# Merged heads stored as one word, and the last recurrent block's scans placed behind attention's first maxima

## The chip, the cores and the metric

The kernel runs on one core of a Trainium2 chip. The metric is device time in microseconds (us) of one execution; lower is better. A core has five engines, each with its own instruction queue that it works through in order: TensorE (PE in the profile, with its weight loads as PEld), VectorE (DVE), ScalarE (ACT), GpSimd (POOL) and SyncE (SP), which here only issues transfers. All transfers run on the core's 16 DMA engines.

## The reference, cut to what matters

One layer of a hybrid encoder over 16 + 1024 tokens of 1024 features. An attention branch (8 query heads of 128, 2 key/value heads) and a recurrent branch (8 blocks of 128 channels, scanned forward and backward) are gated, added, projected and added to the residual; a feed-forward follows.

```python
rnn = (rg_lru(xc, ..., reverse=False) + rg_lru(xc, ..., reverse=True))
rnn = rnn.astype(x.dtype) * jax.nn.gelu(gr)
attn = bidirectional_gqa(q, k, v)        # softmax(q k^T) v, 1024 queries over 1040 keys
g_attn, g_rnn = sigmoid(g_merge) halves
mix = g_attn * attn + g_rnn * rnn
h = h + mix @ w_out[l]
hn = rmsnorm(h, norm2_g[l])
h = h + (silu(g) * u) @ w_ffn_out[l]     # g, u = halves of hn @ w_ffn_in[l]
```

## The kernel before, in words

Fp32 products are made on TensorE from two words per number: `split` writes a rounded high word on ACT (a copy into fp32r, L96) and the low word, the difference, on DVE or POOL (L97). A product is then three matmuls (`mm3`, L102 to L104).

**Recurrent part.** A loop over 8 channel blocks makes projections, gates and decays, and calls `scans(b, ri, aa, tg)`: square roots on ACT (L501), then on DVE for each direction a product (L506) and a scan (L509), then the sum of both directions (L511) and the product with `tg` (L512), and a store to `rm_d[b]` in DRAM (L513). For the last block, b = 7, this is the last work on DVE ahead of attention, and `load_head(0)` has brought in the first query head (`qh`).

**Attention.** For head h and query tile i of 128 queries (64 tiles), `emit_scores` makes scores on PE in one of two PSUM buffers `S0`, `S1` (nine matmuls), their negated maximum `nm` on DVE (L585), the exponential `p` with its sum on ACT (L588), the reciprocal on DVE, and `PP`, the normalised tile as high and low fp16 words (ACT L594, L595; DVE L597). `PP` has a ring of 3 buffers. A DMA transpose, issued by SP (L600), brings `PP` into `PT`. Two tiles make a pair u; `emit_pv`, called up to two pairs later, runs 25 matmuls (`pv`, L611), multiplies by the attention gate on DVE (L613) and adds the recurrent part on POOL (L614), both in a page `gar` that `load_gar` filled from `rm_d`. The gate projections of the coming head (`gap`, L636 to L638) fill PE between score tiles.

**Merged heads.** `emit_pv` splits each 128x256 result into `mst` (ACT, POOL) and stores the two words to `mix_d` (256 KB, L618). `load_mix(kh, c)` later brings the two words of up to 4 heads and half of the tokens into pages `M`, two transfers issued by POOL (L650): four calls, two of them inside the last heads by the table `ahead`, two behind them. The first half of the output projection (`oph`, L677 to L679, with `load_wout` L656 and `load_h` L668 ahead of it) begins beside head 7, then the second half and the norm follow.

**What sets the order.** The code is recorded in this order and a scheduler places instructions on each engine; pools with rings (`pages`, a shared ring of page tiles; `rawp`, three staging tiles `raw`) give a buffer back when its last reader is done. SP issues transposes, loads and stores in one queue, in order: an instruction of SP that waits holds back all behind it.

Of the kernel before, what the change touches and what calls it, by code (L numbers as in the profile page):

```python
# [19 lines left out]
T = 1024  # L20
# [3 lines left out]
NH = 8  # L24
# [18 lines left out]
def tile_hybrid_encoder_block(  # L43
# [73 lines left out]
    rm_d = [dram.tile([128, T], F32, name=f"rm_d{b}") for b in range(NB)]  # L117
    mix_d = [dram.tile([2, 4, 128, T], F32, name=f"mix_d{kh}") for kh in range(2)]

# [377 lines left out]

    def scans(b, ri, aa, tg):
        for r in range(2):
            rr = ri[r][:, 0, (0 if r == 0 else NM):NK]  # L500
            S.activation(out=rr, in_=rr, func=AF.Sqrt)  # L501
        for r in range(2):
            p = ri[r]
            lo = 0 if r == 0 else NM
            rr, ii, a1 = p[:, 0, lo:NK], p[:, 1, lo:NK], aa[:, r, lo:NK]
            V.tensor_tensor(out=ii, in0=ii, in1=rr, op=ALU.mult)  # L506
            if r:
                rr, ii, a1 = rr[:, ::-1], ii[:, ::-1], a1[:, ::-1]
            V.tensor_tensor_scan(out=rr, data0=a1, data1=ii, initial=0.0, op0=ALU.mult, op1=ALU.add)  # L509
        hf, hb = ri[0][:, 0, NM:NK], ri[1][:, 0, NM:NK]  # L510
        V.tensor_tensor(out=hf, in0=hf, in1=hb, op=ALU.add)  # L511
        V.tensor_tensor(out=hf, in0=hf, in1=tg, op=ALU.mult)  # L512
        SP.dma_start(out=rm_d[b], in_=hf)  # L513
# [10 lines left out]
    for b in range(NB):  # L524
        sg = gm_project(b, next_block())
        tg = pb.tile([128, T], F32, name="tg")
        gr = gr_project(b, next_block(), sg, tg)
# [9 lines left out]
        else:  # L537
            q = load_head(0)
        scans(b, ri, aa, tg)

# [23 lines left out]
    SB = [ps2.tile([128, 3, 512], F32, name=f"S{i}") for i in range(2)]  # L564
    PP = [p2.tile([128, KPAIR], F16, bufs=1, name=f"PP{i}") for i in range(3)]
    for p in PP:
# [5 lines left out]
    def emit_scores(h, i, q):  # L572
# [3 lines left out]
        s = SB[n % 2]  # L576
        pair = PP[n % 3]
        if n < 2:
# [5 lines left out]
        nm = small.tile([128, 1], F32, name="nm")  # L584
        V.tensor_reduce(out=nm, in_=s[:, :, 0:KC], axis=AX.XY, op=ALU.max, negate=True)  # L585
        p = p2.tile([128, 3, KC], F32, name="p")
# [11 lines left out]
        if i % 2 == 0:  # L598
            PT[h, i // 2] = p2.tile([128, 17, 256], F16, name="PT")
        SP.dma_start_transpose(  # L600
            out=PT[h, i // 2][:, :, 128 * (i % 2):128 * (i % 2) + 128], in_=pair,
        )

    def emit_pv(h, u, gar):
# [9 lines left out]
        G.tensor_tensor(out=gar[:, 1, c], in0=gar[:, 0, c], in1=gar[:, 1, c], op=ALU.add)  # L614
        if h < NH - 1 or u >= 2:
            st = p2.tile([128, 2, 256], F32R, name="mst")
            split(gar[:, 1, c], st[:, 0], st[:, 1], G)
            SP.dma_start(out=mix_d[h // 4][:, h % 4, :, c].rearrange("l d t -> d l t"), in_=f32(st))  # L618
        elif u % 2 == 1:
            cs = slice(256 * u - 256, 256 * u + 256)  # L620
            split(gar[:, 1, cs], M[0][1][0][:, 3], M[1][1][0][:, 3])
# [22 lines left out]

    def load_mix(kh, c):

        k = 3 if kh and not c else 4
        for hl in range(2):
            M[hl][kh][c] = page([128, 4, 512], F32R, f"M{hl}{kh}{c}")
            G.dma_start(out=M[hl][kh][c][:, 0:k], in_=mix_d[kh][hl, 0:k, :, 512 * c:512 * c + 512].rearrange("h d t -> d h t"))  # L650

# [33 lines left out]
    def out_steps():  # L685
# [8 lines left out]
    ahead = {  # L694
        (6, 4): [(load_mix, 0, 0)],
        (6, 6): [(load_wout, 0, 0), (load_wout, 1, 0)],
        (6, 7): [(load_h, 0, page, [0])],
        (7, 2): [(load_h, 0, page, [1])],
        (7, 3): [(load_wout, 0, 1)],
        (7, 4): [(load_mix, 1, 0)],  # L700
        (7, 5): [(load_wout, 1, 1)],
# [3 lines left out]
    for h in range(NH):  # L705
        for i in range(8):
            emit_scores(h, i, q)
            if i == 1 and h + 1 < NH:
# [463 lines left out]
```

## Time and profile before

| | |
|---|---|
| time, median of 3 runs | 1540.17 us (1540.11 to 1542.09) |
| profiled run: its own time | 1543.0 us |
| its span, first to last instruction | 1541.2 us |
| mean granted TensorE clock | 0.988 |
| PE busy | 1484.2 us, 96% of the span |
| DVE, ACT, POOL busy | 71%, 48%, 21% |
| DMA, mean of the span | 150 GB/s |

PE is nearly always busy, so a microsecond is won only where PE stands idle or runs at its lower clock. In the page's 40 slices PE is full (9 tenths) in most; lower digits stand at the very start, around 500 us, between 690 and 810 us and around 900 us. The DMA row of the same slices reads 9 from about 540 to 810 us, which is attention, and 4 or less in most slices before.

### The profile page before, as it was taken

How to read it: one execution, taken by the hardware profiler on the slowest of the kernel's cores; microseconds unless marked ns; L12 is line 12 of the kernel's file. 1: busy time of each engine (PE TensorE's matmuls, PEld its weight loads, DVE VectorE, ACT ScalarE, POOL GpSimd, SP SyncE). 2: the span in 40 equal slices, each digit the busy share in tenths (PEclk: the TensorE clock that was granted, in tenths of full speed). 3: DMA queues.
4: the chain of work that ended last, by engine and by line, in shares of the span. 5: the costliest groups of instructions: out<-in, count | busy, mean ns of one | idle time of the engine just before them, and what ended most of it. 6: DMA issues, size and time to landing. Idle time of an engine off the chain costs nothing. (4 is left out here: it accounts for less than half of the span.)

```text
span 1541.2 us, 20211 instructions
## 1 busy us (share of the span) xinstructions
PE 1484.2 (96%) x7323; PEld 1241.6 (81%) x7323; DVE 1101.1 (71%) x1712; ACT 743.1 (48%) x1264; POOL 325.3 (21%) x243
## 2 busy tenths in 40 slices
PE   6999999999999899997889979999999999999999
PEld 4888888888888788886778857888888888788887
DVE  6888677777776777786764697777777777667562
ACT  5544476677667666666651352322222222364330
POOL 0000000000000544444341253333333333300000
PEclk9999999999999999999999989999999999999999
DMA  6123311122212799999997215444444444699641
GB/s 240 41 77 101 88 33 60 60 62 62 63 55 78 167 201 201 202 199 228 234 228 246 69 40 165 164 157 158 157 157 158 157 158 157 230 378 330 205 149 66
DMA packets 310196, 230.49 MB, mean 150 GB/s; under 512 B 151016, under 2 KB 252352, under 8 KB 310096
## 3 DMA queue, kind: packets, MB, share of 16 engines
q1 hardware_dynamic: 306128, 221.34, 50.9%
q0 software_dynamic: 3968, 7.86, 1.9%
q8 instruction: 57, 0.93, 0.2%
q14 instruction: 43, 0.35, 0.1%
HBM read 137.15 MB, written 56.36 MB: 126 GB/s over the span
## 5 line engine op out<-in xcount | busy, mean ns | idle before, releaser
L96 ACT ACTIVATE wS<-s 128x512 fp32r<-128x512 f32 x88 | 53.2, 628 | 169.2 <-DVE s L880 51.6
L597 DVE SCALAR_TENSOR_TENSOR PP<-p,pr,PP 128x1024 f16<-128x1024 f32 (+1 forms) x128 | 119.4, 986 | 20.2 <-ACT PP L594 20.0
L96 ACT ACTIVATE pw<-pr 128x1024 fp32r<-128x1024 f32 x77 | 81.0, 1061 | 104.8 <-PE po L1088 63.4
L1086 PE MATMUL po<-pw 128*128 128x512 f32 x308 | 120.4, 391 | 1.5 <-ACT pw L96 1.5
L1087 PE MATMUL po<-pw 128*128 128x512 f32 x308 | 120.6, 391 | 0.8 <-DVE pw L97 0.8
L1088 PE MATMUL po<-pw 128*128 128x512 f32 x308 | 120.3, 391 | 0.0
L97 DVE TENSOR_TENSOR pw<-pr,pw 128x1024 fp32r<-128x1024 f32 x77 | 94.0, 1251 | 36.1 <-ACT pw L96 29.7
L611 PE MATMUL pv<-PT,vt 128*128 128x256 f16 x800 | 97.7, 281 | 17.6 <-DMA PT<-PP 16.9
L588 ACT ACTIVATE p<-S,nm 128x1044 f32<-128x1044 f32 x64 | 72.2, 1129 | 68.2 <-DVE nm L585 65.7
L611 PEld LDWEIGHTS <-vt 128*128 128x128 f16 x800 | 78.0, 101 | 33.5 <-issue 18.3
L97 DVE TENSOR_TENSOR wS<-s,wS 128x512 fp32r<-128x512 f32 x88 | 70.5, 818 | 16.9 <-ACT wS L96 16.0
L594 ACT ACTIVATE PP<-p,pr 128x1040 f16<-128x1040 f32 x64 | 73.9, 1155 | 15.2 <-DMA PT<-PP 10.3
L585 DVE TENSOR_REDUCE nm<-S 128x1 f32<-128x1044 f32 x64 | 76.8, 1231 | 2.1 <-PE S L104 2.1
L433 POOL MEMSET xrp<- 128x2 f32 x8 | 0.9, 108 | 349.8 <-DVE xc L440 349.8
L102 PE MATMUL S<-kT,qh 128*128 128x348 f32 (+1 forms) x192 | 63.6, 331 | 6.7 <-ACT p L588 6.4
L1086 PEld LDWEIGHTS po<-pw 128*128 128x128 f32 x308 | 58.1, 189 | 14.1 <-ACT pw L96 1.9
L1087 PEld LDWEIGHTS po<-pw 128*128 128x128 f32 x308 | 58.2, 189 | 13.0 <-DVE pw L97 1.1
L1088 PEld LDWEIGHTS po<-pw 128*128 128x128 f32 x308 | 58.2, 189 | 12.2
L103 PE MATMUL S<-kT,qh 128*128 128x348 f32 (+1 forms) x192 | 62.1, 323 | 0.0
L104 PE MATMUL S<-kT,qh 128*128 128x348 f32 (+1 forms) x192 | 62.0, 323 | 0.0
L97 DVE TENSOR_TENSOR wA<-raw,wA 128x512 fp32r<-128x512 f32 x60 | 50.3, 842 | 15.9 <-ACT wA L96 15.9
L103 PE MATMUL xr<-xn,wblk 128*128 128x264 f32 (+1 forms) x192 | 61.4, 320 | 0.0
(308 smaller groups left out, 4467.0 us busy)
## 6 DMA issues: line engine op xcount, KB each, us to landing
raw<-in_w_ffn_in_dram SPq DMA_DIRECT2D x47, 512.0 KB, 4.8
raw<-in_w_in_dram SPq DMA_DIRECT2D x44, 512.0 KB, 4.1
pr<-act_d SPq DMA_DIRECT2D x77, 256.0 KB, 5.3
raw<-in_w_ffn_out_dram SPq DMA_DIRECT2D x22, 512.0 KB, 4.6
wot_d<-bs SPq DMA_DIRECT2D x44, 256.0 KB, 4.5
act_d<-as SPq DMA_DIRECT2D x44, 256.0 KB, 2.0
pr<-wot_d SPq DMA_DIRECT2D x44, 256.0 KB, 5.3
act_d<-act SPq DMA_DIRECT2D x33, 256.0 KB, 3.3
```

Source lines behind the costliest of these rows:

```text
L96: S.activation(out=hi, in_=src, func=AF.Copy)
L97: (eng or V).tensor_tensor(out=lo, in0=src, in1=f32(hi), op=ALU.subtract)
L102: PE.matmul(out=ps, lhsT=lh, rhs=rh, start=(k == 0), stop=False)
L103: PE.matmul(out=ps, lhsT=lh, rhs=rl, start=False, stop=False)
L585: V.tensor_reduce(out=nm, in_=s[:, :, 0:KC], axis=AX.XY, op=ALU.max, negate=True)
L588: S.activation(out=p, in_=s[:, :, 0:KC], func=AF.Exp, bias=nm, accum_out=den)
L594: S.activation(out=pair[:, 0:NK], in_=pf, func=AF.Copy, scale=r)
L597: V.scalar_tensor_tensor(out=pair[:, o:o + e - a], in0=pf[:, a:e], scalar=r, in1=pair[:, a:e], op0=ALU.mult, op1=ALU.subtract)
L611: PE.matmul(out=ps, lhsT=vt[:, j, hl, vs], rhs=pt[:, m], start=(n == 0), stop=(n == len(terms) - 1))
L1086: PE.matmul(out=banks[t], lhsT=lh, rhs=w[:, 0, 1], start=j == 0, stop=False)
L1087: PE.matmul(out=banks[t], lhsT=lh, rhs=w[:, 1, 1], start=False, stop=False)
L1088: PE.matmul(out=banks[t], lhsT=ll, rhs=w[:, 0, 1], start=False, stop=j == NFP - 1)
```

## The change

Two things. First, `scans` becomes a generator that stops after the square roots and after each direction's scan. For blocks 0 to 6 it is run through at once. For block 7 only the square roots run in place; the product and scan of one direction, of the other, and the sum, product and store are each placed behind the maximum of one of attention's first score tiles. The tile `tg` of that block becomes a page (`tgl`), and `PP` gets a fourth buffer. Second, `emit_pv` no longer makes `mst`: it stores the fp32 result straight from `gar`, for two pairs together (128x512 words, 256 KB), so 15 stores in place of 30. `load_mix` loads up to two heads' fp32 words into a `raw` tile through SP and splits them there, on ACT and on POOL (c = 0) or DVE (c = 1), into the same pages `M`: 8 loads of at most 512 KB in place of 8 of 768 or 1024 KB.

```diff
-    mix_d = [dram.tile([2, 4, 128, T], F32, name=f"mix_d{kh}") for kh in range(2)]
+    mix_d = [dram.tile([4, 128, T], F32, name=f"mix_d{kh}") for kh in range(2)]
...
     def scans(b, ri, aa, tg):
...
             S.activation(out=rr, in_=rr, func=AF.Sqrt)
+        yield
         for r in range(2):
...
             V.tensor_tensor_scan(out=rr, data0=a1, data1=ii, initial=0.0, op0=ALU.mult, op1=ALU.add)
+            yield
...
-        tg = pb.tile([128, T], F32, name="tg")
+
+        tg = page([128, T], F32, "tgl") if b == NB - 1 else pb.tile([128, T], F32, name="tg")
...
-        scans(b, ri, aa, tg)
+        late = scans(b, ri, aa, tg)
+        next(late)
+        if b + 1 < NB:
+            for _ in late:
+                pass
...
-    PP = [p2.tile([128, KPAIR], F16, bufs=1, name=f"PP{i}") for i in range(3)]
+    PP = [p2.tile([128, KPAIR], F16, bufs=1, name=f"PP{i}") for i in range(4)]
...
-        if h < NH - 1 or u >= 2:
-            st = p2.tile([128, 2, 256], F32R, name="mst")
-            split(gar[:, 1, c], st[:, 0], st[:, 1], G)
-            SP.dma_start(out=mix_d[h // 4][:, h % 4, :, c].rearrange("l d t -> d l t"), in_=f32(st))
-        elif u % 2 == 1:
-            cs = slice(256 * u - 256, 256 * u + 256)
+        if u % 2 == 0:
+            return
+        cs = slice(256 * u - 256, 256 * u + 256)
+        if h < NH - 1 or u == 3:
+            SP.dma_start(out=mix_d[h // 4][h % 4, :, cs], in_=gar[:, 1, cs])
+        else:
             split(gar[:, 1, cs], M[0][1][0][:, 3], M[1][1][0][:, 3])
...
-    def load_mix(kh, c):
-
-        k = 3 if kh and not c else 4
+    def load_mix(kh, c, eng=None):
+
         for hl in range(2):
             M[hl][kh][c] = page([128, 4, 512], F32R, f"M{hl}{kh}{c}")
-            G.dma_start(out=M[hl][kh][c][:, 0:k], in_=mix_d[kh][hl, 0:k, :, 512 * c:512 * c + 512].rearrange("h d t -> d h t"))
+        for k in range(0, 4, 2):
+            n = 1 if kh and not c and k else 2
+            raw = raw_tile([128, 2, 512])[:, 0:n]
+            SP.dma_start(out=raw, in_=mix_d[kh][k:k + n, :, 512 * c:512 * c + 512].rearrange("h d t -> d h t"))
+            split(raw, M[0][kh][c][:, k:k + n], M[1][kh][c][:, k:k + n], eng)
...
-            emit_scores(h, i, q)
+            found = emit_scores(h, i, q)
+            if not h:
+                with tc.issue_after(found.ins):
+                    next(late, None)
```

DVE at the start of attention, before; `nm<-S_...` is the maximum of a score tile, `ri` holds the recurrent block, `den` and `pr` belong to the softmax sum:

```order
L506 TENSOR_TENSOR ri<-ri 128x1040
L506 TENSOR_TENSOR ri<-ri 128x1024
L509 SCALAR_TENSOR_TENSOR ri<-aa,ri 128x1040
L509 SCALAR_TENSOR_TENSOR ri<-aa,ri 128x1024
L511 TENSOR_TENSOR ri<-ri 128x1024
L585 TENSOR_REDUCE nm<-S_4498 128x1
L512 TENSOR_TENSOR ri<-ri,tg 128x1024
L585 TENSOR_REDUCE nm<-S_4499 128x1
```

DVE at the same place, now:

```order
L593 TENSOR_REDUCE nm<-S_4491 128x1
L508 TENSOR_TENSOR ri<-ri 128x1040
L511 SCALAR_TENSOR_TENSOR ri<-aa,ri 128x1040
L598 TENSOR_SCALAR den<-den 128x1
L599 RECIPROCAL pr<-den 128x1
L593 TENSOR_REDUCE nm<-S_4492 128x1
L605 SCALAR_TENSOR_TENSOR PP_4493<-p,pr,PP_4493 128x1024
L605 SCALAR_TENSOR_TENSOR PP_4493<-p,pr,PP_4493 128x16
L598 TENSOR_SCALAR den<-den 128x1
L508 TENSOR_TENSOR ri<-ri 128x1024
L599 RECIPROCAL pr<-den 128x1
L511 SCALAR_TENSOR_TENSOR ri<-aa,ri 128x1024
```

The first maximum now stands ahead of both scans, the second behind one of them; the sum (now L514) follows the third, the product with `tgl` (L515) the fourth.

POOL near the end of head 4, before; `M` are the pages of merged heads, `mix_d_92` their DRAM copy of heads 0 to 3:

```order
L614 TENSOR_TENSOR gar<-gar 128x256
L97 TENSOR_TENSOR mst<-gar,mst 128x256
L650 DMA M_6918<-mix_d_92 128x4x512
L650 DMA M_6920<-mix_d_92 128x4x512
L614 TENSOR_TENSOR gar<-gar 128x256
```

SP now, where the same heads are loaded:

```order
L661 DMA raw<-mix_d_92 128x2x512
L608 DMA_TRANSPOSE PT<-PP_4493 128x17x128
L608 DMA_TRANSPOSE PT<-PP_4494 128x17x128
L661 DMA raw<-mix_d_92 128x2x512
L628 DMA mix_d_93<-gar 128x512
L608 DMA_TRANSPOSE PT<-PP_4495 128x17x128
```

The two transfers of POOL's queue have become two loads in SP's, each in front of a pair of transposes.

SP where the last of heads 4 to 6 is loaded, now (`mix_d_93` holds heads 4 to 7):

```order
L628 DMA mix_d_93<-gar 128x512
L661 DMA raw<-mix_d_93 128x512
L668 DMA raw<-in_w_out_dram 128x2x512
L608 DMA_TRANSPOSE PT<-PP_4495 128x17x128
L608 DMA_TRANSPOSE PT<-PP_4496 128x17x128
```

The load reads what the store in front of it writes, so it waits for that store's landing, and the two transposes stand behind it in the queue.

## Rows read from the trace of the kernel before

**Rows 1.** Waits, 480 to 900 us: engine line <- awaited: total, times, longest us.

```profile
PE pv L611 <- DMA PT<-PP: 16.9, 5, 7.8
PE S L102 <- ACT p L588: 6.4, 7, 3.6
```

**Rows 2.** Windows: length, busy of PE, PEld, DVE, ACT, POOL (counts); clock; DMA share; GB/s.

```profile
500.00:520.00 20.00, 16.10 (x76) 13.36 (x75) 16.87 (x20) 10.59 (x17) 12.92 (x8) 0.93 0.61 158
...
700.00:760.00 60.00, 48.62 (x312) 42.20 (x309) 42.26 (x66) 36.61 (x61) 25.16 (x21) 0.94 1.13 245
760.00:800.00 40.00, 34.48 (x206) 29.12 (x207) 32.27 (x48) 25.61 (x40) 20.96 (x14) 0.91 1.10 233
800.00:880.00 80.00, 80.00 (x400) 66.31 (x399) 38.60 (x79) 16.46 (x33) 14.75 (x15) 1.00 0.53 158
1150.00:1541.00 391.00, 385.15 (x1691) 317.93 (x1689) 253.90 (x305) 133.32 (x169) 64.78 (x41) 1.00 0.57 197
```

**Rows 3.** Timeline of PE around 500 us: start, us, what [idle before <- releaser].

```profile
499.62 0.39 PE L636 MATMUL gap<-xn,wblk 128*128 128x512 f32 x1
...
507.50 0.43 PE L102 MATMUL S<-kT,qh 128*128 128x348 f32 x1 [0.27 <-ACT p L588]
...
518.41 0.66 PE L102 MATMUL S<-kT,qh 128*128 128x348 f32 x1 [3.64 <-ACT p L588]
```

**Rows 4.** Timeline of DVE at the start of attention.

```profile
496.75 2.38 DVE L506 TENSOR_TENSOR ri<-ri 128x1040 f32<-128x1040 f32 x2 [2.11 <-ACT ri L501]
499.05 4.50 DVE L509 TENSOR_TENSOR_SCAN ri<-aa,ri 128x1040 f32<-128x1040 f32 x2
503.58 1.45 DVE L511 TENSOR_TENSOR ri<-ri 128x1024 f32<-128x1024 f32 x1
504.96 1.23 DVE L585 TENSOR_REDUCE nm<-S 128x1 f32<-128x1044 f32 x1
506.11 2.92 DVE L512 TENSOR_TENSOR ri<-ri,tg 128x1024 f32<-128x1024 f32 x1
...
512.66 3.23 DVE L597 SCALAR_TENSOR_TENSOR PP<-p,pr,PP 128x1024 f16<-128x1024 f32 x4 [0.83 <-ACT PP L594]
```

**Rows 5.** Timeline of ACT at the start of attention.

```profile
517.14 1.13 ACT L588 ACTIVATE p<-S,nm 128x1044 f32<-128x1044 f32 x1 [2.57 <-DVE nm L585]
```

**Rows 6.** A window of 5 us behind PE's wait, columns as in rows 2.

```profile
520.00:525.00 5.00, 5.00 (x19) 4.41 (x19) 3.58 (x4) 3.03 (x6) 0.33 (x1) 0.61 0.52 97
```

**Rows 7.** Timeline of PE, 715 to 800 us: three of its waits for transposed tiles.

```profile
724.41 4.97 PE L611 MATMUL pv<-PT,vt 128*128 128x256 f16 x25 [7.78 <-DMA PT<-PP]
...
760.74 2.89 PE L611 MATMUL pv<-PT,vt 128*128 128x256 f16 x25 [2.74 <-DMA PT<-PP]
781.33 5.49 PE L611 MATMUL pv<-PT,vt 128*128 128x256 f16 x25 [3.69 <-DMA PT<-PP]
```

**Rows 8.** Timeline of SP's queue around 700 us.

```profile
697.96 5.01 SPq L600 DMA_TRANSPOSE PT<-PP  x2
...
707.42 12.26 SPq L600 DMA_TRANSPOSE PT<-PP  x2
```

**Rows 9.** Timeline of POOL around 709 us.

```profile
709.01 1.84 POOL L650 DMA_DIRECT2D M<-mix_d  x2
```

**Rows 10.** DMA issues, 520 to 800 us: count, KB each, median us to landing.

```profile
mix_d<-mst SPq DMA_DIRECT2D x28, 256.0 KB, 3.6
...
M<-mix_d POOLq DMA_DIRECT2D x2, 1024.0 KB, 10.8
...
M<-mix_d POOLq DMA_DIRECT2D x2, 768.0 KB, 8.3
raw<-in_w_ffn_in_dram SPq DMA_DIRECT2D x3, 512.0 KB, 5.0
```

**Rows 11.** Instructions of tile mst: count, ns min/median/max, first and last start.

```profile
L97 POOL TENSOR_TENSOR mst<-gar,mst x30: 727/1309/1675, 531.6 to 821.9; 128x256 fp32r<-128x256 f32 x30
```

More of the change, by code (lines that the diff above doesn't have):

```diff
@@ L576, in emit_scores @@
         s = SB[n % 2]
-        pair = PP[n % 3]
+        pair = PP[n % 4]
         if n < 2:
@@ L584, in emit_scores @@
         nm = small.tile([128, 1], F32, name="nm")
-        V.tensor_reduce(out=nm, in_=s[:, :, 0:KC], axis=AX.XY, op=ALU.max, negate=True)
+        found = V.tensor_reduce(out=nm, in_=s[:, :, 0:KC], axis=AX.XY, op=ALU.max, negate=True)
         p = p2.tile([128, 3, KC], F32, name="p")
@@ L602, in emit_scores @@
         )
+        return found
     def emit_pv(h, u, gar):
@@ L694, in tile_hybrid_encoder_block @@
     ahead = {
-        (6, 4): [(load_mix, 0, 0)],
+        (6, 4): [(load_mix, 0, 0, G)],
         (6, 6): [(load_wout, 0, 0), (load_wout, 1, 0)],
@@ L699, in tile_hybrid_encoder_block @@
         (7, 3): [(load_wout, 0, 1)],
-        (7, 4): [(load_mix, 1, 0)],
+        (7, 4): [(load_mix, 1, 0, G)],
         (7, 5): [(load_wout, 1, 1)],
```

## The prediction, made before the changed kernel ran

> **What bounds the kernel now.** I read the page first: PE is busy for 96% of the span, so only what stands between PE and its next matmul counts. The windows then say where that is: in the attention part, 16.10 of the 20 us from 500 us, 48.62 of the 60 us from 700 us and 34.48 of the 40 us from 760 us are busy, while 800 to 880 us is full [rows 2]. So the change has about 3.9 + 11.4 + 5.5 = 20.8 us of idle PE there to work on. The waits say for whom: from 480 to 900 us PE waits 16.9 us for transposed tiles, in 5 waits, and 6.4 us for ACT's exponential, in 7 waits, the longest 3.6 us [rows 1]. Each long wait is followed by matmuls at a lower clock: behind the wait of 3.64 us a score matmul takes 0.66 us where the same one took 0.43 us [rows 3], and the next 5 us have a granted clock of 0.61 [rows 6]; behind waits of 7.78 and 3.69 us the 25 `pv` matmuls take 4.97 and 5.49 us, behind one of 2.74 us they take 2.89 us [rows 7]. That is the lower of the two levels, 1.2 GHz against 2.4 GHz. A wait that goes therefore gives more than its own length. The work before the last recurrent block's scans, and the stretch behind 808 us, are the same in both kernels.
>
> **Part A, the scans behind the first maxima.** The first score tile is done when PE turns to gate matmuls, at 499.62 us [rows 3], but DVE takes its maximum at 504.96 us, behind two scans of 4.50 us together and the sum of 1.45 us; another 2.92 us of product stand ahead of the second maximum [rows 4]. All later exponentials run late by that. PE pays at its fifth tile, with 3.64 us of idle time [rows 3], then the half clock: 1.59 us up to 520 us at half speed is 0.8 us, and 5.00 us at 0.61 is 1.95 us [rows 6]. So A can give 3.64 + 2.75 = 6.4 us at most.
> In the new order the chain on DVE from 499.8 us is: maximum 1.23, product and scan 1.19 + 2.25 (half of the two in a row each), maximum 1.23, the low words of `PP` 0.8 (a quarter of 3.23 holds a small one too; two take 1.6 for two tiles), product and scan 3.44, maximum 1.23, with some 0.6 for the small softmax steps [rows 4]. That is 12.0 us: the third maximum ends at 511.8 us and its exponential, 1.13 us [rows 5], at 513.0 us. PE wanted it at 518.41 - 3.64 = 514.8 us, so the wait that cost most is gone. What is late next: the fourth maximum stands behind `PP` 0.8 and the sum, 1.2 to 1.45 us, and ACT's split of the next query head waits for that sum on ACT's in-order queue, with the fourth exponential behind it. I put that exponential's end near 519 us, 2 us later than PE can use it, and take 6.4 - 2 = **4.5 us** (rounded), between 2 and 6.4. The store of the recurrent block moves in SP's queue from ahead of all transposes to between the second and the third; the DMA engines still have room there (share 0.61 [rows 2]), so I cost it at nothing; were that cover gone it would be a store's landing, some 4 us by the 256 KB ones [rows 10].
>
> **Part B, merged heads as one word.** Between 700 and 808 us the DMA engines are the limit: their share is 1.13 and 1.10 [rows 2] (over 1 since two queues' packets overlap). The worst wait, 7.78 us at 724 us, follows POOL's two loads of `M` at 709.01 us [rows 9]: beside them SP needs 12.26 us for a pair of transposes that took 5.01 us at 698 us [rows 8]. How much time bytes cost: from 1150 to 1541 us 197 GB/s take a share of 0.57 [rows 2], so 197 / 0.57 = 345 GB/s for all engines; an estimate, which leaves out what small packets cost.
> Counted at that rate in this stretch: the loads of `M` fall from 2 x 1024 + 2 x 768 KB [rows 10] to half, 1.83 MB, 5.3 us; of the 256 KB stores 11 become 5 or 6, 1.44 MB, 4.2 us; three loads of feed-forward weights of 512 KB [rows 10] move behind the stretch, since `raw` has its three buffers in use, 4.6 us; the first merged heads are now loaded ahead of 700 us, 3.0 us. Against that, the loads of the other half of the tokens, 1.57 MB, come into it: 4.6 us more. Net 12.5 us less work for the engine that limits.
> PE's loss there is its idle time of 11.4 + 5.5 = 16.9 us, plus the slow `pv` groups, 4.97 - 2.89 and 5.49 - 2.89 = 4.7 us [rows 7]; 21.6 us is the upper bound. If only the burst at 709 us goes and new waits eat the rest, it is about 3 us. I take **12 us**, by the byte count.
> On the engines: POOL loses 30 splits of 1.31 us, 39 us [rows 11], ACT 30 copies; ACT gets 8 splits of the loaded words and DVE four, some 1.2 us each by the 1040-wide products [rows 4]. None is a term of its own. The two on DVE ahead of the last gate products, and those on ACT ahead of the norm, lie in 800 to 880 us, where DVE is busy for 38.60 of 80 us and ACT for 16.46 [rows 2]; without that room each costs PE its 1.2 us. Where ACT's splits stand ahead of an exponential in the last heads, they wait for a landed load; that is the rival below. The fourth `PP` buffer lets ACT go on while a transpose reads; it hides transfers and has no time of its own.
>
> **Part C.** Fewer stores between 530 and 700 us and the fourth `PP` buffer act on the short waits for the exponential: 6.4 - 3.64 = 2.8 us [rows 1, 3]. I take **1 us**, from 0 to 2.8.
>
> **The sum.** 4.5 + 12 + 1 = 17.5 us. The profiled run took 1543.0 us against a span of 1541.2 us and would take 1525.5 us; the median of before is 1540.17 us, so I forecast 1522.7 us. Lower bound of the time 1540.2 - (6.4 + 21.6 + 2.8) = 1509 us; with A and B at their lower ends, 2 + 3, 1535 us.
>
> **Rivals.**
> 1. *The loads come ahead of the transposes in one queue.* Before, POOL's 2 MB ran beside the pair: 5.01 us plus 2.1 MB at 345 GB/s, 6.1 us, is 11.1 us, near the 12.26 us seen [rows 8]. Now each 512 KB load (1.5 us at that rate) is issued in front of a pair, four of them within the tight stretch. If a pair starts only when the load ahead is through, 4 x 1.5 = 6 us of B's gain are lost: 1528.7 us. The Trainium skill, "DMA: Bandwidth & Descriptors", section "Queues, rings and completion order", says that each DMA engine takes packets in turn from the queues that have work, and works through one queue's own in order. By that the old load shared the engines with the pair and the new one goes ahead of it. The doubled pair agrees with the first half; no row here shows the second.
> 2. *The transposes themselves hold PE back.* If their small packets limit, and not bytes, B gives its 3 us only, and all is about 6 us with some of A: 1534 us. For it: `pv` waits came also away from POOL's loads, 2.74 us at 760.74 us [rows 7].
> 3. *All waits and slow clocks go.* 1509 us. Against it: something is late next at each place above.
> 4. *Nothing that can be measured.* PE's idle time only moves to the next wait, as A's fourth exponential and the stores: 1537 to 1543 us.
> 5. *Slower, by waits in order on SP.* SP's loads of merged heads wait for the landing of the store directly ahead, 3.6 us [rows 10], or for a `raw` buffer, and hold the transposes behind them, at four places; ACT's split of such a load holds an exponential. Each such wait is as long as the one at 781 us, 3.69 us, and brings the slow `pv` group of 2.6 us [rows 7]: 6.3 us. Two are 12.6 us, three 19 us, more than the 17.5 us: it decides from the third. All four: 1540.2 - 17.5 + 25 = 1548 us. Against it: transposes are issued one or two pairs ahead of their `pv`, which covers part of each.
>
> **How the numbers follow.** Forecast, 1514 to 1526 us: 0.42. Rival 1, 1526 to 1532: 0.18. Rival 2, 1532 to 1537: 0.15. Rival 3, below 1514: 0.10. Rival 4: 0.07. Rival 5: 0.08. The range 1508 to 1537 us takes in all but rivals 4 and 5 and the lowest tail, some 0.83. A difference of 0.2%, 3.1 us, is about what a measurement of this kernel can tell from none: faster than 1537.1 us 0.85, within 0.07, slower 0.08.
>
> **What would show it.** A is right if PE's timeline has no wait of over 2.5 us near 515 us and the clock stays at 1.0 up to 530 us. B is right if from 700 to 808 us PE's waits for transposed tiles fall from 16.9 us to some 5 us, no `pv` group takes over 3 us, and the DMA share falls below 1.05. Rival 1 shows as pairs of transposes that take longer directly behind a load; rival 5 as gaps in SP's queue between a store and the load of the same heads, with `pv` late behind them. It is wrong if idle time appears behind 808 us, by the feed-forward weights that are now loaded later, or if ACT stands before a split while a score tile waits.

## The result, and the profile after

The changed kernel takes 1528.05 us (1526.91 to 1528.59, 4 runs) against 1540.95 us for the one before on the same chip: 12.9 us less, ratio 0.991 with an interval of 0.9897 to 0.9923. Forecast were 1522.7 us and 17.5 us less, so the time lies in the range, 5 us above the forecast. The terms of the sum came out differently from what the total suggests.

The windows of the changed kernel (length, busy time of PE, PEld, DVE, ACT, POOL with counts, granted clock, DMA share, GB/s):

```profile
500.00:520.00 20.00, 18.56 (x94) 15.87 (x94) 19.11 (x21) 11.94 (x19) 5.10 (x4) 1.00 0.48 116
520.00:540.00 20.00, 16.30 (x106) 13.70 (x105) 17.97 (x23) 12.24 (x20) 8.96 (x6) 1.00 0.91 223
...
700.00:760.00 60.00, 53.55 (x335) 47.09 (x334) 45.60 (x73) 39.63 (x64) 25.92 (x17) 0.94 0.96 217
760.00:800.00 40.00, 35.85 (x199) 30.11 (x198) 25.55 (x42) 19.42 (x30) 13.99 (x8) 0.96 1.07 229
800.00:880.00 80.00, 80.00 (x403) 66.43 (x402) 48.25 (x92) 25.20 (x46) 14.72 (x13) 1.00 0.34 116
```

Against [rows 2], PE has 2.5 us more in the first window and 4.9 and 1.4 us more in the late two. But the 20 us from 520 us now hold 3.7 us without work; in the profile of the run named `before_again` below that window is full. PE's waits from 480 to 900 us in the changed kernel (total, times, longest, in us):

```profile
PE S L102 <- ACT p L596: 9.4, 7, 2.4
PE hT L802 <- DVE y L138: 7.2, 2, 5.5
PE pv L620 <- DMA PT<-PP: 4.5, 4, 1.9
PE gap L645 <- ACT gar L551: 4.3, 1, 4.3
```

The waits for transposed tiles fell from 16.9 to 4.5 us, [rows 1]. Those for the exponential rose from 6.4 to 9.4 us, and a new one of 4.3 us, for ACT's gate, has come. The 7.2 us of `hT` belong to the norm and are no change: the kernel before has the same two waits, the longer one just behind 900 us. In the late heads alone, from 700 to 808 us, the waits for transposed tiles fell from

```profile
PE pv L611 <- DMA PT<-PP: 15.8, 4, 7.8
```

before to this:

```profile
PE pv L620 <- DMA PT<-PP: 1.0, 1, 1.0
```

**A row of the profile before that belongs to no kernel.** In the profile before, PE stood at the start of the down projection, long after attention:

```profile
1325.31 0.49 PE L1086 MATMUL po<-pw 128*128 128x512 f32 x1 [1.51 <-ACT pw L96]
1326.57 0.80 PE L1087 MATMUL po<-pw 128*128 128x512 f32 x1 [0.77 <-DVE pw L97]
```

With the slow matmuls behind them this is 4.2 us, and none of the other traces has them. So the kernel before was run once more, without any edit, for its trace alone.

> The kernel before, for its trace alone. The trace of before has two waits of 1.51 and 0.77 us at the start of the down projection (1325 us) that no other trace so far has, with the same order of instructions there. If they belong to that one execution, they are absent here and PE runs from 811 us to the end without a shift against the kernel after; if they belong to the program, they are here again, about 4 us in all.

Measured: 1540.77 us, span 1539.0 us, and at that place no wait:

```profile
1325.38 0.39 PE L903 MATMUL S4B<-B,wS 128*128 128x512 f32 x1
1325.61 0.39 PE L1086 MATMUL po<-pw 128*128 128x512 f32 x1
```

The 4.2 us belong to that one execution. Its profiled time was 1543.0 us where the medians of this kernel in five sessions are 1538.4 to 1541.0 us. From here on, `before_again` is the trace that others are compared with.

**The path.** PE works through 64 score tiles in the same order in all kernels. The start of a tile, less its start in `before_again`, tells what was won or lost up to there (us; h and i as in S(h,i); differences of starts in PE's timeline; the last column is the difference of the spans):

| kernel | S(0,0) | S(0,4) | S(1,4) | S(5,4) | S(6,2) | S(7,0) | S(7,4) | span |
|---|---|---|---|---|---|---|---|---|
| kernel before, first trace | -1.2 | -1.2 | -0.2 | -1.0 | -2.0 | -1.5 | -2.9 | +2.2 |
| changed kernel | -0.4 | -4.8 | +2.5 | -4.5 | -8.8 | -7.0 | -9.3 | -12.4 |
| e1_late | 0.0 | -4.3 | +3.3 | +2.4 | +1.1 | +1.9 | +2.3 | +4.1 |
| e2_mix | -0.5 | -0.5 | -0.4 | -8.1 | -16.9 | -11.2 | -13.5 | -15.3 |
| e3_pp3 | -0.8 | -5.2 | +3.2 | -3.4 | -6.5 | -4.7 | -7.5 | -8.1 |
| e4_dve | +0.2 | -4.1 | +0.6 | -7.1 | -16.9 | -12.6 | -16.1 | -15.7 |
| e5_page | +0.1 | +0.1 | +0.3 | -7.5 | -16.2 | -11.1 | -13.1 | -13.7 |
| e6_both | +0.2 | -3.0 | -2.1 | -9.8 | -19.5 | -11.1 | -13.1 | -13.6 |
| e7_sum | -0.5 | -3.7 | +2.0 | -5.7 | -13.5 | -8.8 | -10.8 | -12.1 |
| e8_dummy | -0.1 | -0.1 | 0.0 | -0.7 | -7.9 | -2.0 | -5.1 | -6.7 |
| e9_defer | -0.5 | -0.5 | -0.5 | -8.1 | -16.8 | -11.1 | -13.6 | -13.4 |
| e10_best | -0.6 | -3.7 | -2.7 | -10.4 | -19.3 | -15.1 | -17.4 | -17.9 |
| e11_lateq | -0.5 | -4.8 | +2.2 | -5.6 | -14.5 | -10.3 | -12.9 | -12.1 |

The first line compares two traces of one kernel: they stay within about 1 us of each other up to S(5,4) and differ by up to 2.9 us behind it, so a smaller difference between two single traces shows nothing. The changed kernel wins 4.3 us up to its fifth tile, loses 7.2 us up to the thirteenth, wins 7.0 us in heads 1 to 5 and 7.9 us behind them.

### The profile page after: what moved, and what is told of

Read it like the earlier page. It is cut to its first block, busy times and chain, and to the rows that moved or that the text cites. A ratio compares the mean times of both kernels' runs of the same rounds, so it can differ in the third digit from the quotient of the medians.

```text
span 1526.6 us, 20094 instructions
## 1 busy us (share of the span) xinstructions
PE 1478.5 (97%) x7323; PEld 1239.4 (81%) x7323; DVE 1098.1 (72%) x1716; ACT 739.8 (48%) x1242; POOL 283.6 (19%) x210
## 5 line engine op out<-in xcount | busy, mean ns | idle before, releaser
L605 DVE SCALAR_TENSOR_TENSOR PP<-p,pr,PP 128x1024 f16<-128x1024 f32 (+1 forms) x128 | 114.7, 952 | 13.4 <-ACT PP L602 12.6
L620 PE MATMUL pv<-PT,vt 128*128 128x256 f16 x800 | 93.0, 273 | 4.9 <-DMA PT<-PP 4.5
L1101 PEld LDWEIGHTS po<-pw 128*128 128x128 f32 x308 | 57.8, 188 | 12.1
```

The lines of the kernel that those rows point to most:

```text
L605: V.scalar_tensor_tensor(out=pair[:, o:o + e - a], in0=pf[:, a:e], scalar=r, in1=pair[:, a:e], op0=ALU.mult, op1=ALU.subtract)
L620: PE.matmul(out=ps, lhsT=vt[:, j, hl, vs], rhs=pt[:, m], start=(n == 0), stop=(n == len(terms) - 1))
L1101: PE.matmul(out=banks[t], lhsT=lh, rhs=w[:, 0, 1], start=j == 0, stop=False)
```

## Experiments on the scans

**Each half alone.** `e1_late` is the kernel before with late scans and the page `tgl` alone; `e2_mix` is the changed kernel without them.

```diff
--- e2_mix, against the changed kernel
-        tg = page([128, T], F32, "tgl") if b == NB - 1 else pb.tile([128, T], F32, name="tg")
+        tg = pb.tile([128, T], F32, name="tg")
...
-        late = scans(b, ri, aa, tg)
-        next(late)
...
+        for _ in scans(b, ri, aa, tg):
+            pass
```

> Only the late scans and the page tgl, on the kernel before: two-word stores, POOL's loads of M and three PP buffers stay. Forecast's theory (A is worth 4.5 us and keeps it): 1535 to 1537 us, the 3.64 us wait at the fifth score tile gone, PE's first pv matmuls about 4 us earlier and everything after them too. Rival, read from the trace of after (the gain is there at the sixth tile and is given back by the twelfth, because DVE's low words of PP then stand still beside POOL's splits of the next head's q and weights): fifth and sixth tile 4 to 5 us earlier, head 1 not earlier than in before, 1539 to 1543 us, and at least one PP pair on DVE of over 4 us within 515 to 545 us.

> Only the one-word store and its loads, with four PP buffers; the scans run at once as before. Forecast's theory (B and C without A): 1528 + 4.5 = 1532 to 1533 us. Rival (A gave nothing in the end): 1526 to 1529 us, head 1 starts within 1 us of before, and heads 2 to 7 gain as much as in after, 12 us.

Measured: `e1_late` 1544.06 us against 1539.53 us, ratio 1.0029 (1.0018 to 1.004): the scans alone make the kernel 4.5 us slower (more than either forecast), with the same three waits of PE for the exponential (1.44, 1.15, 1.44 us) that the changed kernel has below. `e2_mix` 1525.49 us against 1539.53 us, ratio 0.9911 (0.9897 to 0.9925): the other half alone gives the whole gain. By these medians late scans beside the one-word store are worth nothing that can be measured (0.991 with, 0.9911 without); by the path they cost 2.9 us at S(1,4) and 2.9 us in the spans.

The forecast gain is there and then lost. PE in the changed kernel, its waits from 515 to 540 us:

```profile
519.31 0.42 PE L102 MATMUL S<-kT,qh 128*128 128x348 f32 x1 [1.44 <-ACT p L596]
...
526.28 0.43 PE L102 MATMUL S<-kT,qh 128*128 128x348 f32 x1 [1.15 <-ACT p L596]
...
530.84 0.43 PE L102 MATMUL S<-kT,qh 128*128 128x348 f32 x1 [1.44 <-ACT p L596]
...
534.31 2.89 PE L620 MATMUL pv<-PT,vt 128*128 128x256 f16 x25 [1.10 <-DMA PT<-PP]
```

The wait of 3.64 us, [rows 3], is gone, and the granted clock is 1.00 from 500 to 540 us. In its place stand four waits of 1.1 to 1.4 us, and two more follow before the thirteenth tile:

```profile
542.63 2.90 PE L620 MATMUL pv<-PT,vt 128*128 128x256 f16 x25 [0.51 <-DMA PT<-PP]
...
553.07 2.89 PE L620 MATMUL pv<-PT,vt 128*128 128x256 f16 x25 [1.91 <-DMA PT<-PP]
```

The six are 7.6 us. One of them, at 526.28 us, is followed back to DVE, in the same kernel:

```profile
515.80 1.22 DVE L593 TENSOR_REDUCE nm<-S 128x1 f32<-128x1044 f32 x1
516.95 1.21 DVE L515 TENSOR_TENSOR ri<-ri,tgl 128x1024 f32<-128x1024 f32 x1
518.08 5.62 DVE L605 SCALAR_TENSOR_TENSOR PP<-p,pr,PP 128x1024 f16<-128x1024 f32 x2
```

One pair of low words takes 5.62 us there; the pair at 506.96 us took 1.43 us. POOL at the same time splits the next query head and its gate weights:

```profile
516.98 3.40 POOL L97 TENSOR_TENSOR qh<-raw,qh 128x1024 fp32r<-128x1024 f32 x1 [3.58 <-ACT qh L96]
520.34 3.33 POOL L97 TENSOR_TENSOR wblk<-raw,wblk 128x1024 fp32r<-128x1024 f32 x1
```

The two engines block each other: DVE's pair ends at 523.70 us, as POOL's second split does (523.67 us), and POOL's splits take 3.4 us where one without low words beside it takes 2.41 us (528.01 us in `before_again`). ACT's next exponential waits 4.33 us for DVE there, and PE for that exponential at 526.28 us. The Trainium skill, "SBUF — State Buffer", section "Who interferes with whom", says that VectorE and GpSimd share one pair of ports: a VectorE instruction with two inputs in SBUF and a GpSimd instruction that reads SBUF exclude each other, and the later one stands until the first is through. These rows agree with it.

**Is it POOL?** `e4_dve` moves the query heads' and gate weights' low words, and half of those of `M`, from POOL to DVE, in the changed kernel.

```diff
-        split(raw, q[:, 0], q[:, 1], G)
+        split(raw, q[:, 0], q[:, 1], None if h else G)
...
-        (6, 4): [(load_mix, 0, 0, G)],
+        (6, 4): [(load_mix, 0, 0)],
...
-                w_ga = load_block(COL_GA + 128 * (h + 2), G)
+                w_ga = load_block(COL_GA + 128 * (h + 2))
```

> The changed kernel with the low words of the query heads 1 to 7, of the gate weights of heads 2 to 7 and of the first half of M (two calls) made on DVE in place of POOL; the splits of w_out stay on POOL. Theory 1 (DVE's low words of PP stop while POOL runs a split, and this eats A's gain and makes the 4.27 us wait at 721 us): PP pairs of DVE never over 3.5 us up to 712 us, no wait of PE over 2 us up to 715 us, 1518 to 1524 us. Theory 2 (the loads in SP's queue and the waits in order set these waits): the same waits stay, and DVE has 1.2 us more work per split: 1528 to 1532 us.

Measured: 1526.02 us, ratio 0.9914 (0.99 to 0.9929). The time lies between the two forecasts. From S(0,4) to S(1,4) 4.7 us are given back where it were 7.2 us. But `e11_lateq` below, which has none of these splits on POOL either and the same order of instructions up to here, gives back 7.0 us. The two have nearly the same waits; behind the last one, of 1.83 us, `e4_dve` runs its `pv` group at full clock (2.89 us), and behind 2.02 us `e11_lateq` at half (4.51 us; granted clock 0.61 from 543 to 547 us). So POOL's splits are 0.2 to 2.5 us of the loss, and at least 4.7 us have another cause.

**Fewer pieces late.** `e7_sum` takes the scans at once and only the sum, the product and the store behind the second maximum. It is built on `e5_page` below.

```diff
+        late = scans(b, ri, aa, tg)
+        for _ in range(3):
+            next(late)
...
+            if not h and i == 1:
+                with tc.issue_after(found.ins):
+                    next(late, None)
```

> As the run with the page moved, but of the last recurrent block only the sum, the product with tgl and the store are placed behind the second maximum; both scans run at once, ahead of the first. Theory (what the late scans lose is that 9 us of DVE work stand in front of the maxima of tiles 1 to 5; 2.4 us of it can move without harm): the wait for the exponential at the fifth tile falls from 3.7 us to under 1.5 us, head 1 starts 3 to 5 us earlier than without, 1516 to 1518 us. Rival (any of this block's work behind a maximum is given back in head 0, since the same DVE work is only moved): within 1.5 us of the run with the page moved.

Measured: 1528.69 us, ratio 0.9927 (0.9911 to 0.9943), 2.1 us above `e5_page` in the same session, with overlapping intervals. S(0,4) comes 3.7 us early and S(0,6) 2.0 us late: a `pv` group waits 2.49 us for its transposed tile and then runs at half clock, 4.41 us. So even 2.4 us of DVE's work, put off, cost this trace 1.8 us against `e5_page` at the start of head 1.

**The rest of the loss.** `e11_lateq` adds the late scans to `e10_best` (below), in which POOL does none of those splits for heads 1 to 7.

```diff
-        for _ in scans(b, ri, aa, tg):
-            pass
+        late = scans(b, ri, aa, tg)
+        next(late)
...
+            if not h:
+                with tc.issue_after(found.ins):
+                    next(late, None)
```

> Kernel: as e10_best (query and gate-weight low words on DVE, four late loads), with the last block's scans and sums taken in pieces behind attention's first maxima again. Theory (late scans only reorder DVE's work; what PE gains at its fifth tile it waits for by the start of head 1, with POOL's splits of the queries gone too): the fifth tile starts 1 to 4 us earlier than in e10_best, head 1 starts no earlier, and the time is 1524 to 1528 us, ratio 0.991 to 0.993. Rival (the return in the kernel after came from POOL's splits beside DVE, which are gone here): head 1 starts 3 us or more earlier than in e10_best, and the time is 1520 to 1522 us, ratio near 0.988.

Measured: 1526.77 us against 1538.36 us, ratio 0.9917 (0.99 to 0.9934), where `e10_best` has 0.9911 (0.9894 to 0.9927). The medians do not part the two; the traces do, as the first theory foretold. The fifth tile starts 1.1 us earlier than in `e10_best`, S(1,4) 4.8 us later, and the 4.8 us stay unchanged through six heads. POOL is out of it: the pair of low words takes 1.42 us (517.99 us). PE of `e11_lateq` now waits here:

```profile
519.23 0.43 PE L102 MATMUL S<-kT,qh 128*128 128x348 f32 x1 [1.44 <-ACT p L597]
...
529.54 0.43 PE L102 MATMUL S<-kT,qh 128*128 128x348 f32 x1 [1.64 <-ACT p L597]
...
542.75 4.51 PE L621 MATMUL pv<-PT,vt 128*128 128x256 f16 x25 [2.02 <-DVE pr L600]
```

The second wait is followed back on ACT and SP of the same kernel:

```profile
527.32 1.06 ACT L96 ACTIVATE qh<-raw 128x1024 fp32r<-128x1024 f32 x1 [2.92 <-DMA rm_d<-ri]
528.28 1.11 ACT L597 ACTIVATE p<-S,nm 128x1044 f32<-128x1044 f32 x1
```

```profile
497.67 0.32 SPq L520 DMA_DIRECT2D raw<-q_d  x1
...
519.48 3.90 SPq L609 DMA_TRANSPOSE PT<-PP  x1
523.47 0.53 SPq L516 DMA_DIRECT2D rm_d<-ri  x1
...
524.57 0.93 SPq L520 DMA_DIRECT2D raw<-q_d  x1
```

DMA issues from 515 to 535 us (count, KB each, us to landing):

```profile
rm_d<-ri SPq DMA_DIRECT2D x1, 512.0 KB, 3.8
...
raw<-q_d SPq DMA_DIRECT2D x1, 512.0 KB, 6.7
```

The recurrent block's store now stands in SP's queue behind a transpose. It lands 3.8 us after 523.47 us, at 527.27 us, and ACT's split of a query head (of head 2) starts at 527.32 us. It is the landing that the split waits for, and not its own load: that was issued at 497.67 us, and the load of 524.57 us, for head 3, lands only at 531.3 us. `qh` and `ri` are both pages of the shared ring, so the likely reason is that this `qh` takes the place of `ri`; the rows do not number the places. The exponential of a score tile stands behind the split on ACT. In `e10_best` the store is issued at 508.00 us, ahead of the transposes, and the split of the same head (522.22 us) waits for nothing. So the store that the prediction costs "at nothing" holds back an exponential here. `e4_dve` has the same wait, with 2.71 us; in the changed kernel, whose store is issued at 520.90 us, the split (528.63 us) waits for nothing. The third wait, of a `pv` group, is put down to the reciprocal of a late softmax and costs the clock: 4.51 us for 25 matmuls that take 2.89 us elsewhere.

## Experiments on the merged heads

**The fourth buffer.** `e3_pp3` is the changed kernel with three `PP` buffers.

```diff
-    PP = [p2.tile([128, KPAIR], F16, bufs=1, name=f"PP{i}") for i in range(4)]
+    PP = [p2.tile([128, KPAIR], F16, bufs=1, name=f"PP{i}") for i in range(3)]
```

> The changed kernel with three PP buffers in place of four. If the fourth buffer gives the 6 us that heads 2 to 5 won (theory: ACT's waits for a buffer still read by a transpose, 10.3 us in before, made the exponentials late): 1532 to 1535 us and ACT's waits for PP back above 5 us. If fewer bytes gave them: 1528 to 1530 us, within 2 us of the changed kernel.

Measured: 1534.53 us, ratio 0.9964 (0.9949 to 0.9979). A gain of 5.0 us is left of 12.9; the spans differ by 4.3 us. In the path heads 1 to 5 still win 6.6 us, so the buffer is not what they gain by; most of what is lost lies behind S(5,4), where the changed kernel wins 7.9 us and this one 4.7 us. The time is the one that the theory gave, but its sign is not there: ACT's waits for a `PP` buffer come back with 3.4 us, not above 5.

**Bytes or engines in heads 1 to 5.** `e8_dummy` stores one word, as the changed kernel, with three buffers and no late scans, but makes `mst` on ACT and POOL as before and lets nobody read it.

```diff
+        if h < NH - 1 or u >= 2:
+            st = p2.tile([128, 2, 256], F32R, name="mst")
+            split(gar[:, 1, c], st[:, 0], st[:, 1], G)
```

> The run with only the one-word store, with three PP buffers, and the two-word splits mst of each pair made on ACT and POOL again, but not stored or read: the work of the engines is as in before, the bytes are as in the changed kernel. Heads 2 to 5 tell: with fewer bytes as the cause of the 5 us won there, head 5 starts 4 to 6 us earlier than in before relative to head 2; with POOL's and ACT's missing work as the cause, under 1.5 us.

Measured: 1534.71 us, ratio 0.9968 (0.9956 to 0.9981). Up to S(5,4) it wins 0.6 us where `e2_mix` wins 7.6 us. The bytes saved are the same, and the buffer that `e2_mix` has more is not it (`e3_pp3` wins 6.6 us without), so it is the engines: `mst` on POOL and ACT cost these heads about 7 us, against the 1 us of part C. DVE's low words of `PP` from 560 to 700 us show how (groups by line; count, busy time, mean ns), in `before_again`:

```profile
L597 DVE SCALAR_TENSOR_TENSOR PP<-p,pr,PP 128x1024 f16<-128x1024 f32 x32 | 43.6, 1363 | 6.0 <-ACT PP L594 6.0
L597 DVE SCALAR_TENSOR_TENSOR PP<-p,pr,PP 128x16 f16<-128x16 f32 x32 | 18.4, 577 | 0.0
```

and in `e2_mix`:

```profile
L602 DVE SCALAR_TENSOR_TENSOR PP<-p,pr,PP 128x1024 f16<-128x1024 f32 x34 | 46.2, 1359 | 6.2 <-ACT PP L599 6.2
L602 DVE SCALAR_TENSOR_TENSOR PP<-p,pr,PP 128x16 f16<-128x16 f32 x34 | 11.9, 351 | 0.0
```

The instruction on 16 columns, next to no work, takes 577 ns beside `mst` and 351 ns without; it is 224 ns in `e10_best`, where POOL splits still less. Of the two engines that made `mst` it is POOL, by way of DVE: ahead of the exponentials ACT is not late with copies, it waits for DVE's maximum, 31.6 us in `e2_mix` and this in `before_again` (ACT's waits in the same window: total, times, longest, in us):

```profile
ACT p L588 <- DVE nm L585: 41.3, 16, 3.0
```

PE's waits from 560 to 700 us are 4.1 us for the exponential, in 7 pieces of at most 0.8 us, and 1.3 us for low words in `before_again`; in `e2_mix` there is none, and PE is busy for 140.00 of 140 us.

**Two kinds of stall in the late heads.** In the changed kernel the wait of 7.78 us, [rows 7], is gone, but 4.27 us stand close to its place:

```profile
721.05 0.80 PE L645 MATMUL gap<-xn,wblk 128*128 128x512 f32 x1 [4.27 <-ACT gar L551]
```

This is DVE and POOL again. DVE:

```profile
701.23 5.50 DVE L605 SCALAR_TENSOR_TENSOR PP<-p,pr,PP 128x1024 f16<-128x1024 f32 x4 [0.33 <-ACT PP L602]
...
712.62 5.42 DVE L605 SCALAR_TENSOR_TENSOR PP<-p,pr,PP 128x1024 f16<-128x1024 f32 x4 [0.38 <-ACT PP L602]
```

and POOL, with the new splits of `M`:

```profile
704.34 2.35 POOL L97 TENSOR_TENSOR M<-raw,M 128x1024 fp32r<-128x1024 f32 x1 [1.14 <-ACT M L96]
...
710.50 2.40 POOL L97 TENSOR_TENSOR M<-raw,M 128x1024 fp32r<-128x1024 f32 x1 [3.80 <-ACT M L96]
...
715.06 5.25 POOL L97 TENSOR_TENSOR wo<-raw,wo 128x1024 fp32r<-128x1024 f32 x2 [0.49 <-ACT wo L96]
```

Four low words took 3.23 us at [rows 4] and take 5.4 us here: the first four beside a split of `M`, the second beside an addition of POOL and the splits of `wo`, which the kernel before has too. In `e4_dve`, with those splits on DVE, the wait of 4.27 us is one of 0.93 us and S(6,2) comes at -16.9 us where the changed kernel has -8.8 us. `e2_mix` is also at -16.9 us there, with the splits on POOL, a wait of 1.87 us and a head start of 3.6 us: what meets what depends on the instant.

`e2_mix` then loses 5.7 us up to S(7,0), most of it to the second kind. ACT of `e2_mix`:

```profile
733.44 1.06 ACT L96 ACTIVATE M<-raw 128x1024 fp32r<-128x1024 f32 x1 [6.85 <-DMA mix_d<-gar]
```

The split of the loaded heads waits for the landing of a store of merged heads, out of the page whose place `M` takes; exponentials stand behind it, and PE waits 4.57 us and then takes 0.66 us for a score matmul. The changed kernel has the same wait at 737.78 us with 3.16 us. `e5_page` calls that load one tile later, so that another page is used.

```diff
-        (7, 4): [(load_mix, 1, 0, G)],
-        (7, 5): [(load_wout, 1, 1)],
+        (7, 5): [(load_wout, 1, 1), (load_mix, 1, 0, G)],
```

> The run with only the one-word store (scans at once), and the load of merged heads 4 to 6 called one step later, so that its page M is another one than the gate page of head 5, which stays held until that head's second store has landed. Theory (ACT stands 6.85 us before the split into that page, and the exponential and PE's 4.57 us wait with half clock hang on it): ACT's wait before this split under 2 us, PE's wait at 736 us gone, 1519 to 1522 us against 1525.5. Rival (the wait is for the load itself, which SP issues late and in order): ACT still waits 5 us or more there, 1525 us.

Measured: 1526.57 us, ratio 0.9917 (0.9902 to 0.9932): no gain over `e2_mix`. The 6.85 us are gone, but S(7,0) starts at 744.1 us as before, behind new waits of 1.97 us for the exponential and 2.63 us for a transposed tile.

`e6_both` puts the low words of the queries, the gate weights and `M` on DVE as well.

```diff
-        split(raw, q[:, 0], q[:, 1], G)
+        split(raw, q[:, 0], q[:, 1], None if h else G)
...
-        (7, 5): [(load_wout, 1, 1), (load_mix, 1, 0, G)],
+        (7, 5): [(load_wout, 1, 1), (load_mix, 1, 0)],
```

> As the run above, and the low words of query heads 1 to 7, of the gate weights and of the first half of M on DVE in place of POOL. Theory 1 (DVE's low words of PP stop beside POOL's splits): the 1.87 us wait at 714 us goes and the time is 2 to 4 us below the run above. Theory 2 (DVE becomes the engine that sets the exponentials, by 1.2 us more work per split): the same or up to 4 us above the run above.

Measured: 1527.53 us, ratio 0.9922 (0.9906 to 0.9939). It is 3.3 us ahead of `e5_page` at S(6,2); then ACT's split of `M` waits 2.42 us for its load, `PP` stands behind it, a `pv` group waits 6.68 us at 738.5 us, and S(7,0) comes at 744.05 us again. Three kernels with different leads meet at one instant, with the DMA share at 0.94 to 1.03 from 700 to 760 us. This looked like a limit by transfers.

**Transfers out of the last head.** `e9_defer` is `e2_mix` with 2.6 MB of loads issued behind the last transpose; `e10_best` also takes the low words of query heads 1 to 7 and their gate weights off POOL.

```diff
+        moved[0] = SP.dma_start_transpose(
...
+    with tc.issue_after(moved[0].ins):
+        load_wout(2, 1)
+        load_wout(3, 1)
+        load_mix(0, 1)
...
+    with tc.issue_after(moved[0].ins):
+        load_mix(1, 1)
```

> Kernel: as e2_mix (one-word store, four PP buffers, all scans in place), but two loads of output weights and the two loads of the other half of the merged heads are issued behind the last transpose, some 2.6 MB in five transfers, where they stood between the last pairs of transposes. Theory (the end of attention is set by what the DMA engines carry between 690 and 800 us): 2.6 MB at 345 GB/s are 7.6 us, of which PE gets back about half, so 1519 to 1523 us against 1525.5 us of e2_mix, with no wait of PE for a transposed tile of over 1 us behind 750 us. Rival (the transposes' own small packets set it, or the deferred loads are late for the second half of the projection): 1525 to 1529 us, with waits for those loads at 810 to 830 us.

> Kernel: as e9_defer, and the low words of query heads 1 to 7 and of their gate weights are made on DVE, not on POOL. Theory (POOL's splits hold DVE's low words of PP up for 2 to 3 us each, so exponentials come late in heads 0 and 7; but the end is set by DMA): 2 to 3 us are won in head 0 and stay only if e9_defer has made the DMA engines free at the end: 1517 to 1521 us, 2 us or more below e9_defer. If the DMA engines still set the end, within 1 us of e9_defer. Rival (DVE's extra work in its own queue costs as much as the blocking): 1 to 2 us above e9_defer.

Measured: `e9_defer` 1527.32 us, ratio 0.992 (0.9906 to 0.9935), so the theory's 1519 to 1523 us are missed. Attention does end earlier: its last tile S(7,7) is at -16.8 us where `e2_mix` is at -12.3 us. But the span gains only 13.4 us. The next limit waits there, in `e9_defer`:

```profile
784.53 0.50 PE L687 MATMUL oph<-wo,M 128*128 128x512 f32 x1 [0.88 <-DVE h L692]
...
802.08 0.64 PE L687 MATMUL S<-wo,M 128*128 128x512 f32 x1 [3.37 <-DVE h L692]
```

since DVE's splits of the deferred heads now stand ahead of its additions, the first of them beside POOL:

```profile
795.27 3.17 DVE L97 TENSOR_TENSOR M<-raw,M 128x1024 fp32r<-128x1024 f32 x1 [1.54 <-ACT M L96]
...
799.88 1.23 DVE L97 TENSOR_TENSOR M<-raw,M 128x1024 fp32r<-128x1024 f32 x1 [1.44 <-ACT M L96]
```

`e10_best` has 1524.39 us against 1539.0 us, ratio 0.9911 (0.9894 to 0.9927), 2.9 us below `e9_defer` with overlapping intervals (2 or more were expected, though both stand higher than foretold); it has the shortest span, 1521.1 us, and its head start of 2.2 us from head 0 is kept to the end. It also reaches S(7,0) at 740.07 us, not 744 us. So the instant at which three kernels met is no fixed limit; what made them meet is left open. `e2_mix` and `e10_best` have the lowest medians, but their intervals overlap that of the changed kernel: no version was shown to be faster than it.

## Why the prediction was right, and where its steps failed

**Right in the total, by errors that cancel.** In the traces, with `before_again` as the base, the first twelve tiles lose 2.9 us, the tiles from there to S(5,4) win 7.0 us and the rest 7.9 us; with a start 0.4 us earlier that is 12.4 us. Forecast were 4.5, 1 and 12 us for parts A, C and B. No part has the size that was forecast: that the total lies in the range is luck, while the direction and the fall of the waits for transposed tiles are the prediction's own.

**Part A failed at "what is late next".** The chain on DVE was read rightly, but for one term: a tile's low words are two instructions and take 1.43 us, where the sum has a quarter of 3.23. The third exponential starts at 513.08 us, in time for PE; the fifth tile comes 4.3 us earlier, the clock is kept, ACT's split of the next head waits for the sum, 1.53 us in the changed kernel, and the fourth exponential ends at 519.17 us (forecast: near 519) and costs PE 1.44 us (2 were allowed). There the step stopped. What follows up to the thirteenth tile makes it a loss of 7.2 us: 0.2 to 2.5 us by POOL's splits, the rest by work that is put off within a stretch in which DVE is busy for 19.11 of 20 us. That the rest comes from DVE's late work is argued from the rows; no run takes it apart further. The store that was costed at nothing costs nothing in the changed kernel; where it is issued 3 us later, in `e4_dve` and `e11_lateq`, ACT waits 2.7 and 2.9 us for its landing (3.8 us in `e11_lateq`, where the step gave "some 4 us" as the price). The lower bound of A, a gain of 2 us, did not include a loss, though nothing excluded one; alone, A costs 4.5 us.

**Part C was mis-sized by its cause.** It counted only the short waits for the exponential ("2.8 us") and put them down to stores and the fourth buffer. `e8_dummy` shows that the stores are worth under 1 us there and the removed splits 7 us. The prediction had those 39 us of POOL in hand, [rows 11], and called them no term of their own without a reason. POOL is busy for only 21% of the span, but its idle time is no measure: what counted was what DVE could not do meanwhile. The rows hold the sign of it: the product at 506.11 us takes 2.92 us, [rows 4], and 1.21 us in `e10_best`, where POOL does not split the query head beside it.

**Part B had the right mechanism, and two thirds of the size.** From 700 to 808 us the waits for transposed tiles fell from 15.8 to 1.0 us, where "some 5" were forecast, no `pv` group takes over 3 us, and the DMA share is 0.93 (0.96 from 700 to 760 us, then 1.07; SP's queue alone reads 1.06 there, so a share over 1 does not need two queues, as the prediction has it). `e8_dummy`, which has the bytes and the new loads but neither the fourth buffer nor fewer splits, has waits of 1.1 us there and wins 6.0 us behind S(5,4). The fewer bytes and the loads' move from POOL's queue into SP's came together; no run separates the two. The byte count gives what transfers release; it does not say that PE can take it: in the same stretch PE now waits 5.3 us for the exponential and 4.3 us for the gate, where DVE's low words stand beside splits on POOL, of `M` and of `wo`, or where ACT waits for a store.

**"It hides transfers and has no time of its own"** was wrong of the fourth buffer: without it the gain is 5.0 us in place of 12.9.

**The rivals.** Rival 5 has ACT's split of a load hold an exponential. A split does, but it waits for a store's landing, out of the page that `M` takes: 3.16 us in the changed kernel, 6.85 us in `e2_mix`. For its own load it waits 1.47 us in the changed kernel, at 755.31 us. Of the four places in SP's queue, one ahead of 808 us shows a gap between a store (749.58 us) and the load of the same heads (752.12 us): 1.9 us, and PE's next wait for a transposed tile is 1.0 us. Rival 1 shows weakly. Pairs of transposes in the changed kernel:

```profile
694.41 5.06 SPq L608 DMA_TRANSPOSE PT<-PP  x2
...
703.38 5.92 SPq L608 DMA_TRANSPOSE PT<-PP  x2
...
715.11 6.31 SPq L608 DMA_TRANSPOSE PT<-PP  x2
...
770.60 9.61 SPq L608 DMA_TRANSPOSE PT<-PP  x2
```

Behind loads they take 0.9 to 1.3 us more than the first, against the 12.26 us of [rows 8]; the longest, behind three loads of `w_out`, takes 9.61 us. The waits for transposed tiles are 1.0 us in all there, so little of B's gain went this way. Rival 4 describes part A alone, and the scans' term ends on its far side. Of the two signs of being wrong, "idle time behind 808 us" did not come: 800 to 880 us is full. The other came: at 515.84 us ACT stands 1.53 us before a split, and PE waits 1.44 us for the exponential behind it.

## What to carry to other kernels

Work that is put off within a stretch where its engine is busy all the time is not hidden: follow the whole next window, tile by tile, until the path is steady, before a gain at one tile is counted. Take the cost of an idle-looking engine's instructions from what the neighbouring engine does meanwhile: a row that is twice as long as its fellows is the sign. And let a second trace of the kernel before say which of its waits belong to the program, and how far two traces of one kernel lie apart.

## What the runs showed of the hardware

Two-input instructions of DVE and POOL stand in each other's way: a pair of low words takes 1.42 us with POOL idle and 5.62 us beside two splits of POOL, whose own time goes from 2.41 to 3.4 us; four take 2.77 us with POOL idle (543.36 us in `e11_lateq`) and 5.4 us, and one on 16 columns has a mean of 224 ns with few splits of POOL, 351 ns with some and 577 ns with the most. A maximum read from PSUM kept its 1.23 us beside a split of POOL (510.19 us in `before_again`). And one execution of an unchanged kernel held 4.2 us of waits that its next profile did not have.
